# A hybrid attention and convolution layer: the input projection's tokens cut into 272, 256, 256 and 256, and attention begun one gate tile later

## The chip, the cores and the metric

The kernel runs on one core of one Trainium2 chip. The metric is the device time of one execution in microseconds. The engines spoken of are PE (the matrix engine; PEld is its weight load), DVE (vector), ACT (scalar), POOL (GpSimd) and SP (which here only issues DMA transfers). PE adds products up in PSUM, in banks of 512 float32 per partition; DVE or ACT must empty a bank before PE writes to it again.

## The reference, cut to what matters

One layer of width 1024 on 1024 tokens with 16 meta tokens ahead of them (1040 rows in all). All arrays are float32.

```python
h = concatenate([meta, x], axis=1)                    # 1040 x 1024
h = layer_norm(h, in_ln_g, in_ln_b)
z = h @ w_in + b_in                                   # 3840 columns
q, k, v, c_in, gates = split(z)                       # 512, 128, 128, 1024, 2048
a = swa_sink_attention(q, k, v, sinks, rel_bias)      # window 128, 16 meta keys, 8 q heads, 2 kv heads
y_attn = a @ w_attn_proj
c_val, c_gate = split(c_in)
c = causal_dwconv(c_val * sigmoid(c_gate))            # 31 taps
y_conv = silu(layer_norm(c)) @ w_conv_proj
mixed = sigmoid(g_attn) * y_attn + sigmoid(g_conv) * y_conv
h = layer_norm(ALPHA * h + mixed @ w_out)
up = causal_dwconv(h @ ffn_w_up)                      # 3 taps, 2 x 2816 columns
h = layer_norm(ALPHA * h + (gelu(g) * u) @ ffn_w_down)
return h[:, 16:]
```

## The kernel before, in words

**Products in three terms.** A float32 matrix is split into a high part (a copy rounded to the type fp32r) and a low part (what is left, in fp32r), and a product is high x high + high x low + low x high, three matmuls of 128 x 128 weights against a group of token columns. This is `product` (L296): for each of the 8 chunks of the inner dimension, L300, L304 and L305. For the weights ACT makes the high part `whi` (L269) and DVE the low part `wlo` (L272). Two pairs of `whi` and `wlo` take turns.

**The z stage.** z has 30 tiles of 128 columns: q 0 to 3, k 4, v 5, conv values 6 to 9, conv gates 10 to 13, merge gates 14 to 29. Three tiles (one q, k and v) are made first, while the input is still being normalized (L464 to L538, written apart). The other 27 go through `z_tile` (L314): one weight tile, then for each group of tokens `z_group` (L308) takes one of three PSUM banks (tag "mm"), runs the 24 matmuls, and has an evacuation function empty the bank. The groups are the table `HG`, (0, 272), (272, 656), (656, 1040); q tiles and gate tiles use `TG`, the same with the first 14 columns left out, so 258, 384 and 384. Tokens lie in two tiles in SBUF, `RHO` (inner chunks 0 to 3) and `RHC` (4 to 7), each with eight slots, a high and a low one per chunk; `h0` (L255) says where in the tile a slot's columns begin, and the first three tiles, which write these slots, use it too.

**Evacuation.** A conv gate tile: two ACT instructions for each group (L648 and L649, giving a sigmoid by tanh) into one of the staging slots in the tile `FA` (`stage`, L327). A conv value tile: one DVE instruction (L656), which adds the bias and multiplies by the staged sigmoid into `cin`. A q tile: ACT scales into a staging slot (L352) and copies the high part (L354), DVE makes the low part (L355), both go to a scratch array `qd` in DRAM in rows of 64. A merge gate tile: ACT writes tanh into a staging slot (L672), which goes to the scratch array `sgd`.

**Order of the work.** Instructions are written in program order but placed on their engines by a scheduler that goes by priority numbers (`tc.cur_priority`, `rank`) and dependencies; `after(a, b)` adds that a comes behind b. The z tiles come in this order: conv chunk 1 (gate tile 11, value tile 7) and chunk 0, the q tiles, gate tile 0, and then, beside attention, gate tiles 1, 2, conv chunk 2, gate tiles 3, 4, conv chunk 3, gate tiles 5 to 15. Attention goes in 8 blocks of 128 queries for each of 2 kv heads: the queries come back from DRAM as `qt` (a load), PE makes scores (L836), DVE and ACT the softmax, PE transposes (L872) and multiplies with the values (L885). The scheduler lays these between the matmuls of gate tiles. What holds attention's start is `ahead` (L746): the first score product of the meta queries stands behind a chunk of gate tile 0, chosen by number (`first_chunk + 2 * KC + 5`). DVE does the 31 taps of the convolution (L665) where it has time, the residual's multiplications (L447, by the scale of the first layer norm) at the beginning, and the sum of the convolution's channels for its layer norm; PE takes that sum's mean with a ones matrix (`ps_m`, L908 and L909).

After the z stage come the convolution's layer norm, the two projections (L300 to L305 again, into `ps_p`, by groups of 258, 256, 256, 256), the output projection (`ps_w`), the up projection (L1556) and the down projection (L1700).

Of the kernel before, what the change touches and what calls it, by code (L numbers as in the profile page):

```python
# [23 lines left out]
F = mybir.dt.float32  # L24
R = mybir.dt.float32r
# [4 lines left out]
P = 128  # L30
# [25 lines left out]

PG = [(0, 258), (258, 514), (514, 770), (770, 1026)]


# [41 lines left out]
def tile_hybrid_layer(  # L101
# [40 lines left out]
    FA = arena.tile([P, 6144], F, name="FA")  # L142
    RHC = arena.tile([P, 8320], R, name="RHC")
    RHO = arena.tile([P, 8320], R, name="RHO")
    OB = arena.tile([P, 4 * U], F, name="OB")
# [109 lines left out]
    def h0(k, hl, a, b):  # L255
        g = next(g for g, x in enumerate(HG) if a < x[1])
        x, y = HG[g]
        i, n = (k % 4) * 2 + hl, y - x
        o = i * n + ((6144 if i else 0), 272, 3344)[g]
        return (RHO if k < 4 else RHC)[:, o + a - x:o + b - x]  # L260

# [60 lines left out]

    TG = [(a + U0 if i == 0 else a, b) for i, (a, b) in enumerate(HG)]

    st_next = [0]

    def stage(n, lo=4104, cnt=5):  # L327
        i = st_next[0] % cnt
        st_next[0] += 1
        return FA[:, lo + i * 400:lo + i * 400 + n]  # L330

# [310 lines left out]
    def conv_chunk(c):  # L642
        sig = {}

        def g_evac(g, a, b, ps):
            sig[g] = stage(b - a)

            nc.scalar.activation(sig[g], ps, AF.Tanh, bias=bcol(10 + c), scale=0.5)  # L648
            nc.scalar.activation(sig[g], sig[g], AF.Identity, bias=half_, scale=0.5)  # L649

        z_tile(in_cols(10 + c), HG, g_evac, wt_c1[0] if c == 1 else None)
        cin = cp.tile([P, 16 + T], F, name="cin", tag="cin")
        nc.vector.memset(cin[:, 0:16], 0.0)

        def v_evac2(g, a, b, ps):
            nc.vector.scalar_tensor_tensor(cin[:, 16 + a:16 + b], ps, bcol(6 + c), sig[g], OP.add, OP.mult)  # L656

        z_tile(in_cols(6 + c), HG, v_evac2, wt_c1[1] if c == 1 else None)
        with rank(RK_CONV + c * 100):
            for j in range(TAPS):  # L660
                wc = cdw[:, j * CH + c:j * CH + c + 1]
                if j == 0:
                    nc.vector.tensor_scalar(acc[c], cin[:, j:j + U], wc, cdwb(c), OP.mult, OP.add)
                else:
                    nc.vector.scalar_tensor_tensor(acc[c], cin[:, j:j + U], wc, acc[c], OP.mult, OP.add)  # L665
# [79 lines left out]
    gate_tile(0)  # L745
    ahead = chunks_done[first_chunk + 2 * KC + 5]  # L746

# [5 lines left out]
    for h in range(NH):  # L753
# [3 lines left out]
        nc.tensor.matmul(o, pairs0[g][:, 1, r, :], Kx[g][:, 0, 0:16], start=False, stop=True)  # L757
    s2 = ap.tile([P, NH, 16], F, name="s2")
    nc.vector.memset(s2, 0.0)
# [46 lines left out]
    def weights_out(blocks):  # L806
        a, n = 2 * blocks[0], 2 * len(blocks)
        ps = pat.tile([P, 512], F, name="ps_r", tag="t", bufs=2)
        nc.tensor.transpose(ps[:4 * n, :P], rall[:, a:a + n].rearrange("p n h -> p (n h)"), ident)
        t = ap.tile([24, P], F, name="rt", tag="rt", bufs=2)  # L810
        nc.scalar.copy(t[:4 * n], ps[:4 * n, :P])
        for h in range(NH // 2):
            store(dram(rd, 2 * h * S + a * HD, [[HD, n], [S, 2], [1, HD]]),
                  t[h:4 * n:4].rearrange("p (r q) -> p r q", r=2))
# [77 lines left out]
    tc.cur_priority = RK_Z  # L892
    order = [1, 2, "c2", 3, 4, "c3"] + list(range(5, 16))
    for o in order:
# [40 lines left out]
    def temp(n):  # L935
        return tmp_p.tile([P, 386], F, name="t", tag="t", bufs=6)[:, :n]

# [917 lines left out]
```

## Time and profile before

| | |
|---|---|
| median of 3 runs | 1241.26 us (1241.05 to 1242.42) |
| the profiled execution | 1241.21 us |
| its span | 1239.4 us |
| PE busy | 1228.1 us, 8545 matmuls |
| DVE busy | 1084.9 us, 1846 instructions |
| ACT busy | 579.6 us, 1047 instructions |

A profile line in a timeline gives the start from the span's beginning, the duration, engine, source line, operation, output <- inputs, tile shape, and in brackets how long the engine had been idle before it and what released it. Matmuls overlap one another, so their durations add up to more than the time that they take. A line in the list of waits gives the total in us, how often, and the longest. A line in the chain that ended last gives start, length, engine and a number of instructions in a row.

### The profile page before, as it was taken

To read this page: it belongs to the slowest core of one execution; us is meant where nothing else is said; L and a number is where in the kernel's file an instruction comes from. 1 tells how busy PE (TensorE), PEld (TensorE's weight loads), DVE (VectorE), ACT (ScalarE), POOL (GpSimd) and SP (SyncE) were. 2 spreads that over 40 slices of the span, in tenths; PEclk is the share of its full clock that TensorE was granted. 3 is DMA by queue.
4 is the path that set the end of the run, shared out by engine and by line. 5 is a ranking of instruction groups with operands and counts; after the bars stand their busy time and mean duration, and the time that the engine had idled before them with its cause. 6 is when DMAs were issued, how large, how long until landed. Compare 5 with 4: busy or idle time off the path is not lost.

```text
span 1239.4 us, 21709 instructions
## 1 busy us (share of the span) xinstructions
PE 1228.1 (99%) x8545; PEld 1169.1 (94%) x8545; DVE 1084.9 (88%) x1846; ACT 579.6 (47%) x1047; POOL 13.3 (1%) x11
## 2 busy tenths in 40 slices
PE   9999999999999999999999999999999999999997
PEld 8999999999999999888999999999999998888885
DVE  7899989999978798759899999998999986995697
ACT  7522335664255323344755555455454454544330
POOL 0000000000000010000000000000000000000000
PEclk9999999999999999999999999999999999999999
DMA  7296844412264655222145555544455479987722
GB/s 283 67 300 149 194 122 107 122 46 86 80 164 141 177 164 145 102 87 86 52 171 205 204 179 213 184 174 153 162 203 196 174 247 321 387 322 282 255 85 85
DMA packets 109024, 213.08 MB, mean 172 GB/s; under 512 B 31739, under 2 KB 48683, under 8 KB 108794
## 3 DMA queue, kind: packets, MB, share of 16 engines
q1 hardware_dynamic: 93002, 200.63, 49.3%
q10 hardware_dynamic: 15920, 11.07, 3.0%
q8 instruction: 67, 1.10, 0.4%
q14 instruction: 35, 0.29, 0.1%
HBM read 150.04 MB, written 62.70 MB: 172 GB/s over the span
## 4 chain that ended last, share of the span: by engine, by line
PE 96%; DVE 2%; DMA 1%; issue 0%; ACT 0%; SPq 0%; DVEq 0%
PE px L1556 14%; PE py L1556 9%; PE ps_x L1700 9%; PE ps_z L305 8%; PE ps_z L304 8%; PE ps_z L300 8%; PE ps_z L1700 7%; PE pw L1556 5%; PE pz L1556 5%; PE ps_p L300 2%; PE ps_p L304 2%; PE ps_p L305 2%; PE ps_w L305 2%; PE ps_w L304 2%; PE ps_w L300 2%; PE ps_z L514 2%
## 5 line engine op out<-in xcount | busy, mean ns | idle before, releaser
L665 DVE SCALAR_TENSOR_TENSOR FA<-cin,cols,FA 128x1026 f32<-128x1026 f32 x120 | 152.2, 1279 | 0.9
L305 PE MATMUL ps_z<-RHO,wlo 128*128 128x384 f32 (+2 forms) x324 | 104.1, 321 | 0.0
L300 PE MATMUL ps_z<-RHO,whi 128*128 128x384 f32 (+2 forms) x324 | 103.9, 321 | 0.0
L304 PE MATMUL ps_z<-RHO,whi 128*128 128x384 f32 (+2 forms) x324 | 103.9, 321 | 0.0
L305 PE MATMUL ps_z<-RHC,wlo 128*128 128x384 f32 (+2 forms) x324 | 103.8, 320 | 0.0
L304 PE MATMUL ps_z<-RHC,whi 128*128 128x384 f32 (+2 forms) x324 | 103.7, 320 | 0.0
L300 PE MATMUL ps_z<-RHC,whi 128*128 128x384 f32 (+2 forms) x324 | 103.6, 320 | 0.0
L269 ACT CAST whi<-wr 128x1024 fp32r<-128x1024 f32 x37 | 38.9, 1051 | 91.7 <-PE ps_z L304 71.6
L1366 DVE TENSOR_TENSOR RHO<-wr,RHO 128x512 fp32r<-128x512 f32 x92 | 61.9, 685 | 5.2 <-ACT RHO L1365 5.2
L1365 ACT CAST RHO<-wr 128x512 fp32r<-128x512 f32 x92 | 55.3, 619 | 23.3 <-DVE wr L1383 11.4
L300 PEld LDWEIGHTS ps_z<-RHO,whi 128*128 128x128 f32 x324 | 61.0, 188 | 0.1
L300 PEld LDWEIGHTS ps_z<-RHC,whi 128*128 128x128 f32 x324 | 61.1, 189 | 0.0
L304 PEld LDWEIGHTS ps_z<-RHO,whi 128*128 128x128 f32 x324 | 61.0, 188 | 0.0
L305 PEld LDWEIGHTS ps_z<-RHO,wlo 128*128 128x128 f32 x324 | 61.0, 188 | 0.0
L304 PEld LDWEIGHTS ps_z<-RHC,whi 128*128 128x128 f32 x324 | 61.0, 188 | 0.0
L305 PEld LDWEIGHTS ps_z<-RHC,wlo 128*128 128x128 f32 x324 | 61.0, 188 | 0.0
L1383 DVE TENSOR_TENSOR wr<-wr 128x512 f32<-128x512 f32 x88 | 60.2, 684 | 0.2
L272 DVE TENSOR_TENSOR wlo<-wr,whi 128x1024 fp32r<-128x1024 f32 x35 | 42.7, 1219 | 11.5 <-ACT whi L269 11.1
L672 ACT ACTIVATE FA<-ps_z,cols 128x384 f32<-128x384 f32 (+1 forms) x48 | 26.1, 543 | 48.4 <-PE ps_z L305 44.1
L1568 ACT COPY FA<-px 128x514 f32<-128x514 f32 (+2 forms) x23 | 13.1, 571 | 72.1 <-PE px L1556 72.0
L1365 ACT CAST ws<-wr 128x512 fp32r<-128x512 f32 x60 | 36.1, 618 | 19.3 <-DVE wr L1383 10.7
L1556 PE MATMUL px<-OA,RHO 128*128 128x258 f32 (+1 forms) x336 | 43.9, 279 | 0.0
(468 smaller groups left out, 3478.8 us busy)
## 6 DMA issues: line engine op xcount, KB each, us to landing
wr<-in_w_up_dram SPq DMA_DIRECT2D x44, 512.0 KB, 4.9
wr<-in_w_z_dram SPq DMA_DIRECT2D x30, 512.0 KB, 4.4
fd<-FA SPq DMA_DIRECT2D x44, 256.0 KB, 2.4
OB<-in_w_down_dram SPq DMA_DIRECT2D x19, 512.0 KB
qt<-qd SPq DMA_DIRECT2D x28, 256.0 KB, 3.9
sgd<-FA ACTq DMA_DIRECT2D x32, 192.0 KB, 3.0
td<-OB SPq DMA_DIRECT2D x12, 512.0 KB
sums<-fd SPq DMA_DIRECT2D x12, 512.0 KB, 7.0
```

What stands on the lines that cost most here:

```text
L269: ins = nc.scalar.copy(hi, raw)
L272: return (nc.vector if quick else nc.gpsimd).tensor_tensor(lo, raw, f32(hi), OP.subtract)
L300: ins = nc.tensor.matmul(ps, ah, bh, start=i == 0, stop=False)
L304: nc.tensor.matmul(ps, ah, bl, start=False, stop=False)
L305: last = nc.tensor.matmul(ps, al, bh, start=False, stop=i == n - 1)
L665: nc.vector.scalar_tensor_tensor(acc[c], cin[:, j:j + U], wc, acc[c], OP.mult, OP.add)
L672: nc.scalar.activation(t, ps, AF.Tanh, bias=bcol(14 + i), scale=0.5)
L1365: nc.scalar.copy(hi, src)
L1366: ins = nc.vector.tensor_tensor(lo, src, f32(hi), OP.subtract)
L1383: ins = nc.vector.tensor_tensor(*x)
L1556: ins = nc.tensor.matmul(o, x[:, ks], bmat(sub, q, hl, k), start=first and k + j == 0, stop=k == 3 and j == 2, skip_group_check=not first)
L1700: nc.tensor.matmul(banks[i], l[:, ts], r[:, ws], start=first and a and x + k == 0, stop=z and x == len(ops) - 1 and k == 2, skip_group_che ...
```

## The change

- The 27 z tiles made by `z_tile` go by a new table `ZG`, (0, 272), (272, 528), (528, 784), (784, 1040); `TG` is made from it, so 258, 256, 256, 256. The first three tiles and the split of the input keep their groups `HG`.
- In `RHO` and `RHC`, 8448 columns long (8320 before), the first group's slots begin 14 columns later, at 14 + 272 i (and 6208 columns on for slots 3 to 7); the other 768 columns of a slot now lie in one piece, at 880 + 768 i. Before, the two 384s of a slot lay apart.
- `stage` has 7 slots of 286 columns for groups up to 272, and the 5 of 400 for longer ones; the first two small ones lie elsewhere in `FA`.
- Gate tile 1 is written ahead of attention, and `ahead` is a chunk of gate tile 1 (`first_chunk + 4 * KC + 3`).
- Three smaller buffers: the meta queries' scores share the tag of the block scores, `rt` has 1 buffer in place of 2, the temporary of the convolution's layer norm 5 in place of 6.

```diff
+ZG = [(0, 272), (272, 528), (528, 784), (784, 1040)]
...
-    RHC = arena.tile([P, 8320], R, name="RHC")
-    RHO = arena.tile([P, 8320], R, name="RHO")
+    RHC = arena.tile([P, 8448], R, name="RHC")
+    RHO = arena.tile([P, 8448], R, name="RHO")
...
     def h0(k, hl, a, b):
-        g = next(g for g, x in enumerate(HG) if a < x[1])
-        x, y = HG[g]
-        i, n = (k % 4) * 2 + hl, y - x
-        o = i * n + ((6144 if i else 0), 272, 3344)[g]
-        return (RHO if k < 4 else RHC)[:, o + a - x:o + b - x]
+        i = (k % 4) * 2 + hl
+        if a < 272:
+            o = 14 + i * 272 + (6208 if i > 2 else 0)
+        else:
+            o = 880 + i * 768 - 272
+        return (RHO if k < 4 else RHC)[:, o + a:o + b]
...
-    TG = [(a + U0 if i == 0 else a, b) for i, (a, b) in enumerate(HG)]
-
-    st_next = [0]
-
-    def stage(n, lo=4104, cnt=5):
-        i = st_next[0] % cnt
-        st_next[0] += 1
-        return FA[:, lo + i * 400:lo + i * 400 + n]
+    TG = [(a + U0 if i == 0 else a, b) for i, (a, b) in enumerate(ZG)]
+
+    st_next = [0, 0]
+
+    def stage(n):
+        big = n > 272
+        cnt, size = ((7, 286), (5, 400))[big]
+        o = 4136 + st_next[big] % cnt * size
+        if not big and st_next[0] < 2:
+            o = 3240 + st_next[0] * 280
+        st_next[big] += 1
+        return FA[:, o:o + n]
...
-        z_tile(in_cols(10 + c), HG, g_evac, wt_c1[0] if c == 1 else None)
+        z_tile(in_cols(10 + c), ZG, g_evac, wt_c1[0] if c == 1 else None)
...
-        z_tile(in_cols(6 + c), HG, v_evac2, wt_c1[1] if c == 1 else None)
+        z_tile(in_cols(6 + c), ZG, v_evac2, wt_c1[1] if c == 1 else None)
...
     gate_tile(0)
-    ahead = chunks_done[first_chunk + 2 * KC + 5]
+    gate_tile(1)
+    ahead = chunks_done[first_chunk + 4 * KC + 3]
...
-    s2 = ap.tile([P, NH, 16], F, name="s2")
+    s2 = ap.tile([P, 2, 2, KW], F, name="s2", tag="s", bufs=3)
+    s2 = s2.rearrange("p a b c -> p (a b c)")[:, :NH * 16].rearrange("p (h m) -> p h m", m=16)
...
-    order = [1, 2, "c2", 3, 4, "c3"] + list(range(5, 16))
+    order = [2, "c2", 3, 4, "c3"] + list(range(5, 16))
...
-        return tmp_p.tile([P, 386], F, name="t", tag="t", bufs=6)[:, :n]
+        return tmp_p.tile([P, 386], F, name="t", tag="t", bufs=5)[:, :n]
```

How the instructions stand on the engines, at three places. In these listings a row is the source line, the operation, output <- inputs, size, and how many in a row; `ps_z` is a PSUM bank of a z group, `ps_s` one of scores, `kx_731` the keys of one kv head, `OB` and `xn` the residual, `cin` the convolution's input. Line numbers after the change are those of the changed program, where the product's three lines are L302, L306, L307, the scores L844, the residual L453, the split L274 and the value tile's evacuation L662.

PE, at attention's first block scores; before, in gate tile 0's second group:

```order
L305 MATMUL ps_z<-RHC,wlo 128x258
L300 MATMUL ps_z<-RHO,whi 128x384
L304 MATMUL ps_z<-RHO,whi 128x384
L305 MATMUL ps_z<-RHO,wlo 128x384
...
L836 MATMUL ps_s<-kx_731,qt 128x80 x4
L836 MATMUL ps_s<-kx_731,qt 128x144 x4
```

After, in gate tile 1's second group:

```order
L302 MATMUL ps_z<-RHC,whi 128x256
L306 MATMUL ps_z<-RHC,whi 128x256
L307 MATMUL ps_z<-RHC,wlo 128x256
L844 MATMUL ps_s<-kx_731,qt 128x80 x4
L844 MATMUL ps_s<-kx_731,qt 128x144 x4
L302 MATMUL ps_z<-RHC,whi 128x256
```

The scores moved from behind 8 matmuls of gate tile 0's second group to behind 15 of gate tile 1's, one tile of 96 matmuls later. All 1944 matmuls of 256 columns in the z stage stand so: 976 in a run that a 258 group leads, 325 in one that a 272 group leads, 228 behind transposes, 194 behind scores, 83 behind value products, 96 behind products of the projection, the rest behind others.

DVE, at the value tile of conv chunk 1 (the first value tile); before:

```order
L447 TENSOR_TENSOR xn<-xn,gb 128x1024 x2
L447 TENSOR_TENSOR OB<-OB,gb 128x1024 x2
L272 TENSOR_TENSOR wlo<-wr,whi 128x1024
L447 TENSOR_TENSOR OB<-OB,gb 128x1024 x2
L656 SCALAR_TENSOR_TENSOR cin<-ps_z,cols,FA 128x272
L656 SCALAR_TENSOR_TENSOR cin<-ps_z,cols,FA 128x384 x2
L685 CAST kx_731<-FA 128x8x128
```

After:

```order
L453 TENSOR_TENSOR xn<-xn,gb 128x1024 x2
L453 TENSOR_TENSOR OB<-OB,gb 128x1024 x2
L274 TENSOR_TENSOR wlo<-wr,whi 128x1024
L453 TENSOR_TENSOR OB<-OB,gb 128x1024 x2
L662 SCALAR_TENSOR_TENSOR cin<-ps_z,cols,FA 128x272
L662 SCALAR_TENSOR_TENSOR cin<-ps_z,cols,FA 128x256 x2
L691 CAST kx_731<-FA 128x8x128
...
L693 TENSOR_TENSOR kx_732<-FA,kx_732 64x8x128
L693 TENSOR_TENSOR kx_732<-FA,kx_732 64x8x16
L662 SCALAR_TENSOR_TENSOR cin<-ps_z,cols,FA 128x256
L274 TENSOR_TENSOR wlo<-wr,whi 128x1024
```

The residual's multiplications stand ahead of the first evacuation as before; of the now four evacuations, the last stands behind the work on the keys, and a weight split behind it.

ACT, at the q tiles, before and after; `qsh` is the high part, and the DMA rows are stores that ACT issues:

```order
L352 ACTIVATE FA<-ps_z,qb 128x258
L354 CAST qsh<-FA 128x258
L116 DMA qd<-qsh 128x4x64
L352 ACTIVATE FA<-ps_z,qb 128x384
L354 CAST qsh<-FA 128x384
L116 DMA qd<-qsh 128x6x64
```

```order
L358 ACTIVATE FA<-ps_z,qb 128x258
L360 CAST qsh<-FA 128x258
L117 DMA qd<-qsh 128x4x64
L358 ACTIVATE FA<-ps_z,qb 128x256
L360 CAST qsh<-FA 128x256
L117 DMA qd<-qsh 128x4x64
```

A q tile has four such triples now, with transfers of 4 rows of 64 throughout; SP issues the low parts' transfers in the same number. From the first projection product on, the order on every engine is the same but for a few neighbours that changed places.

More of the change, by code (lines that the diff above doesn't have):

```diff
@@ L809, in weights_out @@
         nc.tensor.transpose(ps[:4 * n, :P], rall[:, a:a + n].rearrange("p n h -> p (n h)"), ident)
-        t = ap.tile([24, P], F, name="rt", tag="rt", bufs=2)
+        t = ap.tile([24, P], F, name="rt", tag="rt", bufs=1)
         nc.scalar.copy(t[:4 * n], ps[:4 * n, :P])
```

## The prediction

> **What bounds the kernel now.** I read the profile's page first, then the list of what TensorE (PE) waited for, then PE's timeline around the groups that the change cuts anew, and last VectorE (DVE) and ScalarE (ACT) where they empty PSUM. The page's head, the clock row and the shares of the chain that ended last:
>
> ```profile
> span 1239.4 us, 21709 instructions
> PE 1228.1 (99%) x8545; PEld 1169.1 (94%) x8545; DVE 1084.9 (88%) x1846; ACT 579.6 (47%) x1047; POOL 13.3 (1%) x11
> PEclk9999999999999999999999999999999999999999
> PE 96%; DVE 2%; DMA 1%; issue 0%; ACT 0%; SPq 0%; DVEq 0%
> ```
>
> PE is busy 99% of the span at a full granted clock, and the chain is PE for 96% of it. All that it waited for in the middle of the program:
>
> ```profile
> PE ps_w L538 <- DVE sel L1089: 1.1, 1, 1.1
> PE ps_h L464 <- DVE xn L428: 0.8, 1, 0.8
> PE ps_s L836 <- DMA qt<-qd: 0.4, 1, 0.4
> PE pw L1556 <- DVE OA L1241: 0.4, 1, 0.4
> PE ps_z L511 <- ACT FA L470: 0.3, 1, 0.3
> ```
>
> That is 3.0 us (1.1+0.8+0.4+0.4+0.3), so the time is the number of matmuls times their pace, and a change can act in two ways: through the pace, or through a new wait of PE. The profiled execution took 1241.21 us (span 1239.4); the median of the runs is 1241.26, so a sum against the profile needs no correction.
>
> **The pace of the group sizes.** A single matmul's listed duration is a latency; the pace is the distance between starts, best read from the first rows of two successive groups (start in us, then duration). A gate tile's two 384-column groups, then its 258-column group:
>
> ```profile
> 331.58 0.34 PE L300 MATMUL ps_z<-RHO,whi 128*128 128x384 f32 x1
> ...
> 339.91 0.28 PE L300 MATMUL ps_z<-RHO,whi 128*128 128x258 f32 x1
> ...
> 342.80 0.34 PE L300 MATMUL ps_z<-RHO,whi 128*128 128x384 f32 x1
> ```
>
> Each group is 8 chunks of 3 matmuls. 48 matmuls of 384 columns take 339.91−331.58 = 8.33 us, 173.5 ns each; 24 of 258 take 2.89 us, 120.4 ns each. Nothing in the z stage has 256 columns yet, but the attention projection does, with the same three-term pattern. Its 256s run at two paces:
>
> ```profile
> 425.10 0.28 PE L300 MATMUL ps_p<-OC,whi 128*128 128x256 f32 x1
> ...
> 428.50 0.28 PE L300 MATMUL ps_p<-OA,whi 128*128 128x258 f32 x1
> ...
> 498.74 0.39 PE L300 MATMUL ps_w<-OA,RHC 128*128 128x512 f32 x1
> 498.97 0.28 PE L300 MATMUL ps_p<-OC,whi 128*128 128x256 f32 x1
> ...
> 500.38 0.39 PE L304 MATMUL ps_w<-OA,RHC 128*128 128x512 f32 x1
> ```
>
> Between the first two rows lie 30 matmuls of 256 columns in 3.40 us: 113.3 ns each. Between the last two lie 12 in 1.41 us: 117.5 ns, and these follow a 512. A 512 itself takes 226.7 ns, twice 113.3 (29.93 us for 132 in the chain's row below). In the up projection each 24 are 12 of 258 and 12 of 256 (2.79 us) or 24 of 256 (2.72 us, 113.3 ns), again fast after the 258s:
>
> ```profile
> 654.35 2.79 PE px L1556 x24
> ...
> 668.25 2.72 PE px L1556 x24
> ...
> 1021.69 29.93 PE ps_z L1700 x132
> ```
>
> **Part 1: 768 columns as three 256s in place of two 384s, 27 tiles.** (8 conv tiles, 3 q tiles, 16 gate tiles.) It removes 48 matmuls per tile and adds 72. At the fast pace 72 x 0.1133 = 8.16 us against 8.33: −0.17 us per tile, x27 = −4.5 us, all of it on PE and so on the path. At the slow pace 72 x 0.1175 = 8.46: +0.13 per tile, +3.5 us. At the 258s' own 120.4 ns, the farthest row, 8.67: +0.34, +9.2 us. I take the fast one, because 19 of the 27 tiles lead with a 258 group, as the fast rows of the up projection do, and the z operands follow each other in the projection's order (chunk by chunk, high, low, high). A slow stretch is plausible where 256s resume after a block's score and value matmuls, which I count as 277 of 1944 in the new order: 277 x 4.2 ns = 1.2 us at most, nothing at least; I take +0.5. The eight conv tiles lead with a 272 group, of which no row shows a 256 behind: 8 x 72 x 4.2 ns = +2.4 us if they went slow, zero if fast; I take zero (their 24 matmuls are as steady as a 258 group's, see the 124.6 ns below) and keep 2.4 as a case.
>
> The Trainium skill has a rule that speaks against this part: "TensorE: Matmul & The Clock Gate", section "Back-to-back issue gap", gives the isolated gap of a warm matmul as N/2.4 + 2.5 ns, a fixed sum for each matmul. By it three 256s cost 327.5 ns and two 384s 325.0, which over 24 x 27 triples is an estimated +1.6 us in place of −4.5. The rows above disagree: 1.5 x 113.3 = 170.0 is less than the 173.5 of one 384, and a 512 is no cheaper per column than a 256.
>
> **Part 2: the first group's slots 14 columns later.** The 272 and 258 groups keep their size and read from another column. Their present paces are 120.4 ns above and, at another offset in the up projection, (2.79 − 12 x 0.1133)/12 = 119.2 ns. The 1.2 ns x 456 matmuls (19 tiles) bounds it at ±0.55 us; I take zero. The slots are written by the same copies earlier; longer tiles alone cost no instruction.
>
> **Part 3: one more PSUM evacuation per tile.** 27 more, and 384-column ones become 256. A gate evacuation on ACT and one of the conv value tiles on DVE (the brackets give the idle time before it), and the dense stretch of DVE (its length, then busy time and instructions of PE, weight loads, DVE, ACT and GpSimd, then clock and DMA):
>
> ```profile
> 347.17 0.58 ACT L672 ACTIVATE FA<-ps_z,cols 128x384 f32<-128x384 f32 x1 [1.38 <-PE ps_z L305]
> 78.22 1.01 DVE L656 SCALAR_TENSOR_TENSOR cin<-ps_z,cols,FA 128x272 f32<-128x272 f32 x2
> 190.00:313.00 123.00, 123.00 (x882) 122.38 (x882) 117.49 (x257) 67.76 (x193) 0.00 (x0) 1.00 0.34 92
> ```
>
> In a regular tile it is ready for the bank 0.6 us after its group; three banks take turns, so it has two more groups of time: now 2.89+4.16 or more, afterwards 2 x 2.72 = 5.4 us. That leaves over 4 us of slack, and the added evacuations (under 0.58 us each, 27 x 0.58 = 16 us on an ACT that is idle for 660) lie beside PE; their extra stores to DRAM go out from ACT's and SP's queues with nobody waiting. Price 0, upper bound a wait where the evacuating engine is late, which is the next item. DVE gets 4 more evacuations (conv value tiles) and 3 more splits (q tiles): some 3 us on an engine that in the densest stretch (the last row, 190 to 313 us) is busy 117.49 of 123.
>
> **Part 4: a new wait in the value tile of conv chunk 1.** There DVE evacuates, and it is late already. Its timeline, and PE's first rows of chunk 1's gate tile, of the value tile and of the tile behind it:
>
> ```profile
> 55.22 4.63 DVE L447 TENSOR_TENSOR xn<-xn,gb 128x1024 f32<-128x1024 f32 x4
> ...
> 75.95 2.34 DVE L447 TENSOR_TENSOR OB<-OB,gb 128x1024 f32<-128x1024 f32 x2
> 56.99 0.37 PE L300 MATMUL ps_z<-RHO,whi 128*128 128x272 f32 x1
> ...
> 68.86 0.29 PE L300 MATMUL ps_z<-RHO,whi 128*128 128x272 f32 x1
> ...
> 71.85 0.34 PE L300 MATMUL ps_z<-RHO,whi 128*128 128x384 f32 x1
> ...
> 80.18 0.29 PE L300 MATMUL ps_z<-RHO,whi 128*128 128x272 f32 x1
> ```
>
> The value tile's 272 group (24 matmuls in 2.99 us, 124.6 ns) ends at 71.85, but its evacuation starts at 78.22, when the residual's multiplications (L447, back to back from 55 us, only weight splits and small copies between) are through; it frees the bank at 78.22+0.49 = 78.71. Now the fourth group behind it, the next tile's first, wants that bank at 80.18: 1.5 us to spare. In the changed kernel the fourth group is the value tile's own last: start 68.86−0.17 = 68.69, +2.99 and 2 x 2.72 = 77.12. DVE's order ahead of it is unchanged, so PE waits 78.71−77.12 = +1.6 us. Bounds: 1.0 if DVE comes half a multiplication earlier, 2.0 if the semaphore and the restart cost 0.4. Queued behind the waiting matmul is only PE itself. DVE then does the second and third group at once; the fourth one's evacuation now stands behind the key halves. Their first and last instructions now, with a weight split between:
>
> ```profile
> 80.99 1.55 DVE L685 CAST kx<-FA 128x1024 fp32r<-128x1024 f32 x4
> 82.51 1.20 DVE L272 TENSOR_TENSOR wlo<-wr,whi 128x1024 fp32r<-128x1024 f32 x1
> 84.80 2.77 DVE L687 TENSOR_TENSOR kx<-FA,kx 64x1024 fp32r<-64x1024 f32 x4
> ```
>
> From 80.99 to 84.80+2.77 = 87.57 are 6.6 us, 1.2 of it the split, which the new order puts behind. So the fourth evacuation is through at 78.7 + 0.9 + 5.4 + 0.5 = 85.5, and its bank is wanted three groups on, at 78.7+2.72+2.99+2.72 = 87.1: 1.6 us to spare, no second wait.
>
> **Part 5: attention begins inside the second gate tile.** The first scores now stall PE:
>
> ```profile
> 136.41 5.32 DMA qt<-qd
> ...
> 141.04 0.34 PE L304 MATMUL ps_z<-RHO,whi 128*128 128x384 f32 x1
> 141.77 1.12 PE L836 MATMUL ps_s<-kx,qt 128*128 128x80 f32 x8 [0.39 <-DMA qt<-qd]
> ```
>
> 141.77−141.04 = 0.73 us where the pace is 0.17: 0.56 us lost, because the transfer lands at 136.41+5.32 = 141.73. In the new order a whole tile, about 11 us, stands between, so this goes: −0.55. What is late next: nothing at that place, since the q tiles' splits gain only one small DVE step and one pair of small transfers per half (5.3 us each at most) inside those 11 us. The other end is that DVE and ACT start the softmax 11 us later. The mean of the convolution is where DVE must be done:
>
> ```profile
> 351.86 0.64 PE L909 MATMUL ps_m<-kx,ones_r 128*128 128x258 f32 x3
> 352.18 3.28 DVE L962 TENSOR_TENSOR FA<-FA,ps_m 128x258 f32<-128x258 f32 x8 [5.13 <-PE ps_m L909]
> ```
>
> DVE idles 5.13 us there, waiting for PE, and PE reaches it 4.5−1.6 = 3 us earlier. DVE's work before it is the same but for 3 us; with 5.5 us idle in the dense stretch it fits. Price 0, bounds 0 to +3. The fewer temporary buffers (6 to 5, 2 to 1) and the 16-meta-query scores in a shared buffer: the list of PE's waits has none there, so 0.
>
> **Sum:** 1241.21 − 4.5 + 0.5 + 1.6 − 0.55 = 1238.3 us.
>
> **Rivals.** (a) *All 256s slow* (the other side): the z groups run at 117.5 ns as after a 512. For it: the 384s of the z stage are slower per column than 512s, so something there may hold that the up projection lacks; against it: every 256 behind a 258. It decides at 173.5/1.5 = 115.7 ns. 1241.21+3.5−0.55+1.6 = 1245.8; with a fixed cost as small as +1.6 us for all triples 1243.9. (b) *The gain is eaten in part*: the conv tiles slow (+2.4), or DVE binding between 190 and 350 us (+2 to +3): 1238.3+2.4 = 1240.7. For it, DVE's 117.49 of 123; against, its 5.13 us idle behind. (c) *The new wait does not come*, because DVE's multiplications run earlier or the bank comes from another group: 1238.3−1.6 = 1236.7; against it, DVE's order there is the same. (d) That the cut changes no pace (1.5 x 256 = 384) leaves −0.55+1.6 = +1.0: 1242.3, counted with (b).
>
> **Chances.** Forecast 0.48 (own range 1237.2 to 1239.6), (a) 0.19, (b) with (d) 0.20, (c) 0.13. A difference of 0.2%, 2.5 us, is what a measurement of this kernel can tell from none: faster lies below 1238.8, which holds (c) and two thirds of the forecast, 0.13+0.32 = 0.45; same is the other third and (b), 0.16+0.20 = 0.36; slower is (a), 0.19. The range goes from 1236.2, under (c), to 1245.0, within (a).
>
> **What will show it.** Gate tiles without attention in them should take 2.89+8.16 = 11.05 us (11.22 now); 11.35 is (a). The list of PE's waits should lose the first scores and gain one of 1 to 2 us in ps_z on DVE cin near 77 us. DVE's idle time before the ps_m subtraction should shrink from 5.13 to about 2 us; if PE waits for ps_m or its inputs instead, it is (b). Wrong altogether would be waits of PE on ACT's evacuations, or on qt later in attention.

## The result and the profile after

The changed kernel takes 1244.96 us (median of 7 runs, 1244.67 to 1245.55); the kernel before, beside it on the same chip, 1241.05 us (7 runs, 1240.32 to 1242.42). The ratio is 1.0034 with a 95% interval of 1.0024 to 1.0044: slower by 0.34%, where 0.24% faster was forecast.

The page of the changed kernel's profile, head and clock row:

```profile
span 1243.7 us, 23087 instructions
PE 1228.5 (99%) x9193; PEld 1169.8 (94%) x9193; DVE 1085.9 (87%) x1853; ACT 588.8 (47%) x1078; POOL 13.2 (1%) x11
PEclk9999999999999999999999999999999999999999
```

PE has the 648 additional matmuls, the clock is granted in full, and PE's busy time hardly differs. Where the span grew is told by the first z product of conv chunk 1 and the first product of the projections, of the kernel before (its first row stands in the prediction) and of the changed one:

```profile
409.16 0.28 PE L300 MATMUL ps_p<-OA,whi 128*128 128x258 f32 x1
```

```profile
56.85 0.38 PE L302 MATMUL ps_z<-RHO,whi 128*128 128x272 f32 x1
...
413.56 0.28 PE L302 MATMUL ps_p<-OA,whi 128*128 128x258 f32 x1
```

The z stage, with attention in it, took 409.16−56.99 = 352.17 us and now takes 413.56−56.85 = 356.71: +4.54 us. The stages behind it last the same within 0.1 us. So "the z stage" below means this stretch, and its length is the sharpest measure of an edit.

What PE waited for in the changed kernel:

```profile
PE ps_z L302 <- ACT FA L678: 1.5, 2, 1.2
PE ps_h L470 <- DVE xn L434: 1.4, 1, 1.4
PE ps_z L302 <- DVE cin L662: 1.3, 1, 1.3
PE ps_s L844 <- DMA qt<-qd: 1.1, 1, 1.1
...
```

Against the list of before there are two new lines in the z stage, on ACT (1.5) and on DVE's `cin` (1.3), and the one on `qt` has grown from 0.4 to 1.1. (The line on `xn`, before the z stage, was between nothing and 1.6 us in the kernels below, whose beginning is the same.)

The pace of gate tiles 7 and 8, where nothing lies between the matmuls; first rows of successive groups:

```profile
311.39 0.28 PE L302 MATMUL ps_z<-RHO,whi 128*128 128x256 f32 x1
...
319.87 0.28 PE L302 MATMUL ps_z<-RHO,whi 128*128 128x258 f32 x1
...
322.75 0.28 PE L302 MATMUL ps_z<-RHO,whi 128*128 128x256 f32 x1
...
330.92 0.29 PE L302 MATMUL ps_z<-RHO,whi 128*128 128x258 f32 x1
```

From 311.39 to 319.87 are 72 matmuls of 256 columns in 8.48 us, 117.8 ns each; from 322.75 to 330.92 the next tile's 72 in 8.17 us, 113.5 ns. Slow and fast tiles alternate, from the first q tile (slow) to gate tile 10, wherever attention does not break in. All undisturbed conv tiles, which begin with a 272 group, are fast.

Sorting the distance from each matmul's start to the next start, over the whole z stage, gives this sum (a steady matmul is one behind the first five of its run):

| term | us |
|---|---|
| 1944 x 113.3 ns in place of 1296 x 173.4 ns | −4.5 |
| steady matmuls slower than their fast pace: 256s 3.1, 272s 0.3, less 0.2 for 258s and what the kernel before had | +3.2 |
| first five matmuls of a group or behind another product | +1.4 |
| waits of PE (4.5 in the distances, 0.6 before) | +4.0 |
| the rest, attention's own products among it | +0.4 |
| sum | +4.5 |

So the gain that was forecast from the pace is there, and is given back twice: about 4.6 us by pace and 4.0 by waits.

### The profile page after: what moved, and what is told of

Same layout as the page of the kernel before. It is cut to its first block, busy times and chain, and to the rows that moved or that the text cites. A ratio compares the mean times of both kernels' runs of the same rounds, so it can differ in the third digit from the quotient of the medians.

```text
span 1243.7 us, 23087 instructions
## 1 busy us (share of the span) xinstructions
PE 1228.5 (99%) x9193; PEld 1169.8 (94%) x9193; DVE 1085.9 (87%) x1853; ACT 588.8 (47%) x1078; POOL 13.2 (1%) x11
## 4 chain that ended last, share of the span: by engine, by line
PE 92%; DVE 3%; DMA 2%; ACT 2%; issue 1%; SPq 0%; ACTq 0%; DVEq 0%
PE px L1564 14%; PE py L1564 9%; PE ps_x L1708 9%; PE ps_z L1708 7%; PE ps_z L302 7%; PE ps_z L306 7%; PE ps_z L307 7%; PE pw L1564 5%; PE pz L1564 5%; PE ps_p L302 2%; PE ps_p L306 2%; PE ps_p L307 2%; PE ps_w L307 2%; PE ps_w L306 2%; PE ps_w L302 2%; PE ps_z L520 2%
## 5 line engine op out<-in xcount | busy, mean ns | idle before, releaser
L302 PE MATMUL ps_z<-RHO,whi 128*128 128x256 f32 (+2 forms) x432 | 121.9, 282 | 2.8 <-ACT FA L678 1.5
L307 PE MATMUL ps_z<-RHC,wlo 128*128 128x256 f32 (+2 forms) x432 | 121.7, 282 | 0.0
L307 PE MATMUL ps_z<-RHO,wlo 128*128 128x256 f32 (+2 forms) x432 | 121.6, 282 | 0.0
L302 PE MATMUL ps_z<-RHC,whi 128*128 128x256 f32 (+2 forms) x432 | 121.5, 281 | 0.0
L306 PE MATMUL ps_z<-RHO,whi 128*128 128x256 f32 (+2 forms) x432 | 121.3, 281 | 0.0
L306 PE MATMUL ps_z<-RHC,whi 128*128 128x256 f32 (+2 forms) x432 | 121.3, 281 | 0.0
L302 PEld LDWEIGHTS ps_z<-RHO,whi 128*128 128x128 f32 x432 | 81.8, 189 | 3.4 <-ACT FA L678 1.9
L302 PEld LDWEIGHTS ps_z<-RHC,whi 128*128 128x128 f32 x432 | 81.9, 189 | 0.0
L306 PEld LDWEIGHTS ps_z<-RHC,whi 128*128 128x128 f32 x432 | 81.4, 188 | 0.0
L306 PEld LDWEIGHTS ps_z<-RHO,whi 128*128 128x128 f32 x432 | 81.4, 189 | 0.0
L307 PEld LDWEIGHTS ps_z<-RHO,wlo 128*128 128x128 f32 x432 | 81.4, 188 | 0.0
L307 PEld LDWEIGHTS ps_z<-RHC,wlo 128*128 128x128 f32 x432 | 81.3, 188 | 0.0
L678 ACT ACTIVATE FA<-ps_z,cols 128x258 f32<-128x258 f32 (+1 forms) x64 | 30.2, 473 | 66.2 <-PE ps_z L307 62.6
L274 DVE TENSOR_TENSOR wlo<-wr,whi 128x1024 fp32r<-128x1024 f32 x35 | 42.7, 1219 | 10.4 <-ACT whi L271 9.7
L1374 DVE TENSOR_TENSOR ws<-wr,ws 128x512 fp32r<-128x512 f32 x60 | 40.4, 685 | 4.0 <-ACT ws L1373 3.9
```

The costliest lines, as they stand in the source:

```text
L274: return (nc.vector if quick else nc.gpsimd).tensor_tensor(lo, raw, f32(hi), OP.subtract)
L302: ins = nc.tensor.matmul(ps, ah, bh, start=i == 0, stop=False)
L306: nc.tensor.matmul(ps, ah, bl, start=False, stop=False)
L307: last = nc.tensor.matmul(ps, al, bh, start=False, stop=i == n - 1)
L678: nc.scalar.activation(t, ps, AF.Tanh, bias=bcol(14 + i), scale=0.5)
L1374: ins = nc.vector.tensor_tensor(lo, src, f32(hi), OP.subtract)
```

## The experiments

Each kernel was timed beside the kernel before on the same chip; the table gives both, the ratio with its 95% interval, and the z stage of the profiled execution (352.17 us in the kernel before, 356.71 in the changed one).

| kernel | median, us | before beside it | ratio | z stage, us |
|---|---|---|---|---|
| changed | 1244.96 | 1241.05 | 1.0034 (1.0024 to 1.0044) | 356.71 |
| e1_offset0 | 1245.53 | 1241.00 | 1.0037 (1.0024 to 1.0050) | 356.91 |
| e2_lead | 1244.87 | 1241.00 | 1.0030 (1.0018 to 1.0041) | 354.76 |
| e3_chunk1_hg | 1243.75 | 1241.00 | 1.0024 (1.0015 to 1.0034) | 354.55 |
| e4_gate1_back | 1245.80 | 1241.00 | 1.0042 (1.0030 to 1.0055) | 358.66 |
| e5_q_hg | 1244.07 | 1240.10 | 1.0030 (1.0019 to 1.0041) | 354.70 |
| e6_offset2 | 1244.12 | 1240.10 | 1.0037 (1.0022 to 1.0051) | 355.17 |
| e7_fewer_waits | 1240.44 | 1240.10 | 1.0004 (0.9994 to 1.0013) | 351.75 |
| e8_held | 1240.21 | 1240.10 | 1.0000 (0.9991 to 1.0010) | 351.36 |
| e9_spare_banks | 1241.24 | 1240.42 | 1.0004 (0.9995 to 1.0013) | 352.10 |
| e10_all_three | 1240.99 | 1240.42 | 1.0004 (0.9996 to 1.0013) | 352.20 |
| e11_and_leads | 1239.63 | 1240.42 | 0.9993 (0.9984 to 1.0002) | 350.53 |
| e12_more_leads | 1238.75 | 1240.41 | 0.9985 (0.9976 to 0.9994) | 350.61 |

The kernels ran on several chips, and the kernel before took 1240.10 to 1241.05 us beside them, so medians are best compared as distances to it: +3.9 us for the changed kernel. The expectations' times are worked out from 1244.96 us, that is beside 1241.05. The ratios of e1 to e6 overlap with that of the changed kernel, so their medians do not tell them apart from it; what they show is in their traces, one execution of each. e7 to e12 are clear of the changed kernel.

The theory was that the pace of a 256 is a state carried from group to group, and that three late arrivals (DVE, the queries, ACT), each brought by the finer cut, make the waits. The rivals: that the slow pace belongs to a place (column, weight buffer, bank), and that the waits come from attention's later begin.

### The first group's slots back at column 0

```diff
-            o = 14 + i * 272 + (6208 if i > 2 else 0)
+            o = i * 272 + (6208 if i > 2 else 0)
```

> The changed kernel (1244.96 us) with the first group's slots 14 columns earlier again (at 272 i, and 6208 columns on for slots 3 to 7); nothing else moves on any engine. Theory A (phase): a 256 runs at 113.3 or 117.8 ns according to the state in which the group ahead ended, and each 258 group turns one state into the other, so tiles alternate; the column offset only sets the 272 groups' pace, which goes from 127.7 back to 124.6 ns (192 x 3.1 ns = 0.6 us): 1244.4 us, tiles still alternate. Rival B (place): the slow state comes from the 258 groups' new column, so all 256s become fast: 1.551 thousand steady 256s lose their 3.1 us, and with the 272s it takes 1241.3 us.

First rows of groups in e1_offset0, a conv tile's 272 and its first 256, then gate tile 7's 256s:

```profile
69.25 0.28 PE L302 MATMUL ps_z<-RHO,whi 128*128 128x272 f32 x1
...
72.25 0.28 PE L302 MATMUL ps_z<-RHO,whi 128*128 128x256 f32 x1
...
311.11 0.28 PE L302 MATMUL ps_z<-RHO,whi 128*128 128x256 f32 x1
...
319.58 0.28 PE L302 MATMUL ps_z<-RHO,whi 128*128 128x258 f32 x1
```

Neither came out. The 272 group is back at 3.00/24 = 125 ns, as theory A had it (at column 14 it was 127.7). But the alternation is gone the wrong way: gate tile 7 takes 8.47 us, tiles 8 and 9 as much, and most 256s are slow, also in three of the four conv tiles ahead of the q tiles; slow steady 256s cost 4.7 us in place of 3.1. So the column of the group ahead does decide the state in which the 256s run, and the 14 columns of the change are worth 1.6 us of pace here. The time hardly moves (z stage +0.2) because the waits and the 272s got shorter by about as much.

### A short matmul ahead of each gate tile's second group

```diff
+        product(ps[:, :b - a], [...],
+                lead=h0(0, 0, a, a + 64) if a == 272 and lead_on[0] else None)
...
+        lead_on[0] = True
         z_tile(in_cols(14 + i), TG, gate_evac)
+        lead_on[0] = False
```

> The changed kernel with one matmul of 64 columns more ahead of the second group of each of the 16 gate tiles (its result is overwritten). Theory A (phase): the interruption resets the state, every gate tile's 256s run at 113.3 ns after a few; 8 slow tiles get 0.3 us each back (2.4), and 16 interruptions cost 0.13 us each (2.1, from the projection's lead: 33 ns and a first 256 of 199 ns): 1244.7 us. Rival C (weight buffers or PSUM banks, which alternate from tile to tile too): slow tiles stay slow, and the interruptions are paid: 1247.0 us.

The same two gate tiles in e2_lead, from the short matmul to the next tile:

```profile
311.49 0.19 PE L300 MATMUL ps_z<-RHO,whi 128*128 128x64 f32 x1
311.51 0.36 PE L302 MATMUL ps_z<-RHO,whi 128*128 128x256 f32 x1
...
319.76 0.29 PE L302 MATMUL ps_z<-RHO,whi 128*128 128x258 f32 x1
...
322.65 0.19 PE L300 MATMUL ps_z<-RHO,whi 128*128 128x64 f32 x1
...
330.93 0.29 PE L302 MATMUL ps_z<-RHO,whi 128*128 128x258 f32 x1
```

8.27 and 8.28 us including the short matmul: both fast, in the same weight buffers and banks as in the changed kernel, where they took 8.48 and 8.17. That rejects the rival with buffers and banks, and shows the state as something that an interruption resets. (In one of the 16 gate tiles, between attention's products at 235 us, the 22 matmuls behind the short one were slow even so.) What the state gives, 1.5 us of slow steady 256s, the interruptions take (about 0.11 us each: 8.28−8.17). That the median, 1244.87 us, is near the 1244.7 expected is in part luck: in this execution the waits for ACT and for the queries were 1.1 and 0.7 us shorter, which is most of the 1.95 us by which the z stage is shorter, and 1.2 us came back behind the z stage, 0.7 of it as waits in the down projection.

### Conv chunk 1 by the old groups

```diff
-        z_tile(in_cols(10 + c), ZG, g_evac, wt_c1[0] if c == 1 else None)
+        z_tile(in_cols(10 + c), HG if c == 1 else ZG, g_evac, wt_c1[0] if c == 1 else None)
...
-        z_tile(in_cols(6 + c), ZG, v_evac2, wt_c1[1] if c == 1 else None)
+        z_tile(in_cols(6 + c), HG if c == 1 else ZG, v_evac2, wt_c1[1] if c == 1 else None)
```

> The changed kernel with conv chunk 1's two tiles by the old groups 272, 384, 384. The wait of the value tile on DVE's evacuation (1.3 us at 78.6) goes; two tiles go back from three fast 256s to two 384s (+0.33): 1244.0 us. Rival: the tiles behind then wait for the same late DVE (as the next tile would for its bank), and the time stays at 1245.0 or above.

The head of PE's waits in e3_chunk1_hg:

```profile
PE ps_z L302 <- ACT FA L678: 1.8, 2, 1.2
PE py L1564 <- ACT OB L1576: 1.2, 1, 1.2
...
```

Behind these are only lines from ahead of the z stage. The wait for DVE is gone and the z stage is 2.2 us shorter, since the wait for the queries went with it. The q tiles are cut here as in the change, so their cut alone does not bring that wait. In this execution 1.2 us came back as a wait in the up projection, far behind the edit; a similar one, 1.4 us, shows in e5. What brings it was not pursued. The median, 1243.75, is close to the 1244.0 expected.

### Attention's begin as before

```diff
-    gate_tile(1)
-    ahead = chunks_done[first_chunk + 4 * KC + 3]
+    ahead = chunks_done[first_chunk + 2 * KC + 5]
...
-    order = [2, "c2", 3, 4, "c3"] + list(range(5, 16))
+    order = [1, 2, "c2", 3, 4, "c3"] + list(range(5, 16))
```

> The changed kernel with gate tile 1 written behind attention again and the meta queries' scores held by a chunk of gate tile 0's third group, as before. If the later begin of that part is what made the waits for the queries (1.1 us at 144) and for ACT (1.5 us at 378 and 385), both go: 1242.4 us. If they come from the cut into more groups, they stay, and it takes 1244.5 to 1245.5 us.

The three waits of the z stage in e4_gate1_back:

```profile
PE ps_z L302 <- ACT FA L678: 1.8, 1, 1.8
PE ps_z L302 <- DVE cin L662: 1.3, 1, 1.3
PE ps_s L843 <- DMA qt<-qd: 1.1, 1, 1.1
```

All three are there, none smaller, and the time is above the range given for this case (1245.8). So the waits come from the cut, not from the moved gate tile. The z stage of this execution is 1.95 us longer than the changed kernel's, and the granted clock explains 1.7 of them. It dropped right behind the wait of 1.8 us on ACT (columns as in the prediction's row of the dense stretch, the clock third from the end):

```profile
386.02:389.43 3.41, 3.41 (x18) 3.41 (x18) 3.22 (x9) 1.16 (x3) 0.00 (x0) 0.50 0.76 187
```

For 3.41 us the clock was half, and the 256s there lie 213 ns apart; elsewhere in the z stage it was granted in full, and slow steady 256s cost 3.1 us, as in the changed kernel. So moving the gate tile changed the pace neither way. That the wait brought the clock down is not shown: the changed kernel waited 1.2 us at the same place and kept it.

### The q tiles by the old groups

```diff
-        z_tile(in_cols(r), TG, q_evac(r))
+        z_tile(in_cols(r), THG, q_evac(r))
```

(`THG` is `HG` without its first 14 columns.)

> The changed kernel with the three q tiles by the old groups 258, 384, 384. Theory (cut): three groups more to evacuate, split and send per q tile are what makes the queries late, so PE's wait for them falls from 1.1 to about 0.4 us (-0.7), while the three tiles' pace changes by less than 0.3 us: 1244.3 us. Rival: the wait depends on when PE gets there alone, and stays at 1.1: 1245.0 us.

```profile
PE ps_s L845 <- DMA qt<-qd: 0.2, 1, 0.2
```

PE's wait for the queries falls from 1.1 to 0.2 us, as the theory has it. But it was gone in e3 too, and is in e7 below, both with the q tiles cut in four, so this run does not show their cut as the cause. The z stage loses 2.0 us rather than 0.7: slow steady 256s cost 1.2 us less (two of the changed kernel's slow tiles are q tiles), and the wait on ACT is 0.4 us shorter. The median is no nearer to the kernel before (+4.0), with 1.4 us back in the up projection.

### The first group's slots at column 2

```diff
-            o = 14 + i * 272 + (6208 if i > 2 else 0)
+            o = 2 + i * 272 + (6208 if i > 2 else 0)
```

> The changed kernel with the first group's slots beginning at column 2 + 272 i in place of 14 + 272 i, so that the 258 groups begin on a multiple of 16 columns, as in the projections, where every 256 behind them ran at 113.3 ns. If the column decides how a group leaves the pace of those behind it: all 256s behind 258 groups fast (-3.1 us of slow steady matmuls, nearly all), 1242.0 us; the conv tiles' 272 groups at column 2 are not known, and if they leave their 256s slow that is +2.3. If the state only flips at each 258 group, whatever its column: 1245 us.

A conv tile, then gate tile 8, in e6_offset2:

```profile
96.44 0.28 PE L302 MATMUL ps_z<-RHO,whi 128*128 128x256 f32 x1
...
104.92 0.28 PE L302 MATMUL ps_z<-RHO,whi 128*128 128x258 f32 x1
...
321.87 0.29 PE L302 MATMUL ps_z<-RHO,whi 128*128 128x256 f32 x1
...
330.04 0.28 PE L302 MATMUL ps_z<-RHO,whi 128*128 128x258 f32 x1
```

Gate tile 8 now takes 8.17 us, and tiles 7 and 9 as much: behind the 258s nothing alternates. The conv tile takes 8.48: the 272 group at column 2 leaves the 256s at the slow pace. Slow steady 256s cost 2.1 us (3.1 in the changed kernel), 1.2 of it in the four conv tiles ahead of the q tiles, so the place as such was worth 1.0 us of pace. The median does not show it: it is 4.0 us above the kernel before, as the rival's 1245 us would be. Until here a place that is always fast behind a 258 would do as well as a state; e10 decides.

### Without the waits: old groups at four tiles, the scores held

```diff
+        z_tile(in_cols(14 + i), THG if i in (12, 13) else TG, gate_evac)
...
+                        if not i:
+                            after(ins, held)      # e8 alone
+    held = chunks_done[first_chunk + 2 * KC + 2]
```

Both have the slots at column 2 and chunk 1 by the old groups.

> As the kernel before it in this list (slots from column 2), and conv chunk 1's two tiles and gate tiles 12 and 13 by the old groups 272 or 258, 384, 384. The waits for DVE (1.3 us at 78.6) and ACT (1.5 us at 378 and 385) go, four tiles cost 0.17 to 0.3 us more: 1.9 us below that kernel, so 1240.1 us if its 256s are fast, 1243.0 if not. Rival: the waits only move to tiles behind, no gain.

> As the kernel before it, and the scores of attention's first block held behind a chunk of gate tile 0's third group, 16 matmuls of 256 later (1.8 us). PE's wait for the queries (1.1 us at 144 in the changed kernel) goes: 1.0 us below that kernel, 1239.1 us if the 256s are fast. Rival: the later softmax brings a new wait of the same size further on: no gain.

In e7_fewer_waits none of the lines on ACT, `cin` and `qt` is left in PE's list, and with 1240.44 us it is 0.3 us above the kernel before. That the expected 1240.1 us was nearly met is luck: it was worked out for fast 256s and a gain of 1.9 us over e6, but slow steady 256s still cost 1.7 us, and the z stage gained 3.4 us, since the wait for the queries went with the other two. In e8_held nothing is left to gain by holding the scores, and 0.2 us is what the median moved, so this run says little on holding them.

### Without the waits: a fourth bank

```diff
     def z_group(wt, g, a, b, evac, spare=None):
         hi, lo = wt
-        ps = pat.tile([P, 512], F, name="ps_z", tag="mm", bufs=3)
+        tag, bufs = spare if spare and g == 3 else ("mm", 3)
+        ps = pat.tile([P, 512], F, name="ps_z", tag=tag, bufs=bufs)
...
+        z_tile(in_cols(6 + c), ZG, v_evac2, ..., ("s", 2) if c == 1 else None)
...
+        z_tile(in_cols(14 + i), TG, gate_evac, spare=("o", 1) if i in (11, 12, 13) else None)
```

> The changed kernel (1244.96 us) with all groups as cut, but a PSUM bank that is idle at the time taken for the fourth group of conv chunk 1's value tile (one of the scores' banks) and of gate tiles 11, 12 and 13 (the attention output's bank), so that four banks take turns there. If a late evacuation and three banks are the cause of the waits on DVE (1.3 us) and ACT (1.5 us): both go, 1242.2 us. If PE's earlier arrival lets the wait for the queries at 144 us grow by what was won at 78 us: 1243.5 us. Rival: the waits come from something else than the bank: 1245.0 us.

PE's waits in e9_spare_banks:

```profile
...
PE ps_s L845 <- DMA qt<-qd: 0.5, 1, 0.5
...
```

With every tile cut as in the change and the slots at column 14, the lines on `FA` L678 and `cin` are gone from the list, and the time is 1241.24 us, 0.8 us above the kernel before in place of 3.9: the waits were most of the slowdown. That is 0.3 us better than expected (1242.2 beside 1241.05), and the wait for the queries shrank too. For the value tile the bank is the cause: DVE begins that evacuation no earlier than in the changed kernel (78.80 us, 78.10 there), and PE no longer waits for it. On ACT the scheduler also laid the table loads differently, so there the bank is not shown alone.

### Everything together, and short matmuls where the pace is slow

```diff
 # e10: slots at column 2, a fourth bank, the scores held
 # e11: and
         sig = {}
+        lead_on[0] = c < 2
...
+        lead_on[0] = False
 # e12: and
+        lead_on[0] = i in (1, 12)
         z_tile(in_cols(14 + i), TG, gate_evac, ...)
+        lead_on[0] = False
```

> The kernel before it with slots from column 2 + 272 i and the first block's scores held 16 matmuls longer: every tile cut as in the change, none of the three waits, and the 258 groups leaving a fast state. Against 1244.96 us: -1.3, -1.5 and -1.1 us of waits and about -2.0 us of slow steady 256s: 1239.1 us, below the kernel before. If the pace alone cannot pay for the cut, it stays at 1241 or above.

> As e10, and a matmul of 64 columns ahead of the second group of the four conv tiles of chunks 1 and 0, whose 272 groups (at column 2) leave a slow state: 4 x (0.32 - 0.12) = 0.8 us less, 1238.3 us. Rival: the interruption costs what it saves, 1239.1 us.

> As e11, with the matmul of 64 columns also ahead of the second group of gate tiles 1 and 12, which run slow in e11 (2 x 72 x 4.4 ns lost): 2 x (0.32 - 0.12) = 0.4 us less, 350.1 us for the z stage (350.5 in e11; 352.2 in the kernel before) and 1.2 us below the kernel before. Rival: the interruptions move the scheduler's order around attention, and other tiles fall into the slow state for it: the z stage takes 350.5 us or more.

Two tiles in e10_all_three, with the slots at column 2 as in e6: the first q tile, then gate tile 8:

```profile
106.73 0.29 PE L302 MATMUL ps_z<-RHO,whi 128*128 128x256 f32 x1
...
114.90 0.28 PE L302 MATMUL ps_z<-RHO,whi 128*128 128x258 f32 x1
...
319.91 0.28 PE L302 MATMUL ps_z<-RHO,whi 128*128 128x256 f32 x1
...
328.39 0.28 PE L302 MATMUL ps_z<-RHO,whi 128*128 128x258 f32 x1
```

The q tile takes 8.17 us, gate tile 8 takes 8.48, and gate tiles 7 and 9 as much: the same column, behind a 258 group each time, gives both. In e6 attention's last product left the 256s at the fast pace, here at the slow one, and the 258 groups behind it hand on the pace that they find. So a pace is carried on, and the place alone does not set it. The pace ahead does not set it alone either: the q tile above is fast behind a conv tile whose 256s were slow. The 258s tell the two cases apart: 24 of them take 2.89 us behind the conv tile and 2.85 us between slow gate tiles.

It cost e10 its gain: no wait in the z stage, 3.6 us of slow steady 256s, and 0.6 us above the kernel before where 2.0 below was expected. e11 has 1.3 us of them left and the shortest z stage, 350.53 us; its ratio still reaches 1. The short matmuls gave 0.8 us of that gain and cost some 0.4 themselves; 1.8 us came behind attention, where gate tiles 7 to 9 and 13 to 15 happened to be fast again. e12 has 0.6 us left; in its profiled execution the wait for the queries is back with 0.4 us, and the z stage is not shorter than e11's, as its rival had it. Its runs are nevertheless the only ones clear of the kernel before: 1238.75 against 1240.41 us, 0.9985 (0.9976 to 0.9994), 1.7 us where 1.2 was expected. Which part of it the two further short matmuls brought is not shown.

## Why the prediction was wrong

**The pace (part 1), mis-sized.** −4.5 was right as the price of fast 256s. The step that failed is the choice that all 256s behind a 258 group are fast, read from the attention and up projections. In the up projection 12 and 24 matmuls stand behind 258s at another column. In the attention projection, where the 113.3 ns was first read, the run of 256s does not stand right behind the 258s; the kernel before has a matmul of 64 columns between them:

```profile
412.05 0.19 PE L298 MATMUL ps_p<-OA,whi 128*128 128x64 f32 x1
412.08 0.36 PE L300 MATMUL ps_p<-OA,whi 128*128 128x256 f32 x1
```

That is the interruption that e2 copied, and it leaves the fast pace. The rows of before could not show that the state is handed on. Slow steady 256s took 3.1 us where 0.5 was set, of the 8.0 us that lie between all fast (−4.5) and all slow (+3.5). (The 0.5 counted the 256s behind scores and value products; the 228 behind transposes, listed in the part on the change, were left out.) Conv tiles, kept as a case, were fast.

**What the sum left out.** The first matmuls behind a change of size or behind another product cost 1.4 us more; no term had them. The 14 columns (part 2) were set to zero with a bound of 0.55; on the 272s alone they cost about 192 x 2.5 ns = 0.5 us, from 125.0 ns in e1 to the 127.5 ns (3.06/24) of this pair of rows of the changed kernel, but their larger effect was on the state.

```profile
93.16 0.29 PE L302 MATMUL ps_z<-RHO,whi 128*128 128x272 f32 x1
...
96.22 0.28 PE L302 MATMUL ps_z<-RHO,whi 128*128 128x256 f32 x1
```

**The evacuations on ACT (part 3), wrong.** "Over 4 us of slack" was worked out from a stretch where ACT had little else. Where the convolution's layer norm runs, ACT's rows of before and of the changed kernel are these:

```profile
372.19 2.09 ACT L995 ACTIVATE FA<-FA,cols 128x258 f32<-128x258 f32 x4
374.18 0.56 ACT L672 ACTIVATE FA<-ps_z,cols 128x384 f32<-128x384 f32 x1
```

```profile
372.63 2.09 ACT L1003 ACTIVATE FA<-FA,cols 128x258 f32<-128x258 f32 x4
374.74 1.28 ACT L991 ACT_TABLE_LOAD   x1
376.03 0.58 ACT L991 ACTIVATE t<-ps_m,eps 128x384 f32<-128x384 f32 x1
376.63 1.28 ACT L678 ACT_TABLE_LOAD   x1
377.93 0.47 ACT L678 ACTIVATE FA<-ps_z,cols 128x256 f32<-128x256 f32 x1
...
379.72 1.28 ACT L991 ACT_TABLE_LOAD   x1 [0.39 <-ACT FA L678]
...
381.62 1.28 ACT L1003 ACT_TABLE_LOAD   x1
...
385.08 0.45 ACT L678 ACTIVATE FA<-ps_z,cols 128x256 f32<-128x256 f32 x1
```

```profile
385.58 0.39 PE L302 MATMUL ps_z<-RHO,whi 128*128 128x256 f32 x1 [1.15 <-ACT FA L678]
```

Before, an evacuation stood right behind the swish activations (L995). Now it stands behind two more table loads and an activation, at 377.93, 3.2 us after the swish ended; ACT is busy from 372.63 to 378.40, 5.8 us and longer than the two groups of 2.7 us for which three banks last, and PE waits 0.3 us. The longer wait, 1.15 us, comes two groups later: the evacuation that it needs starts at 385.08, again behind two table loads, with activations and a weight cast between, and PE's matmul starts when it is through. The Trainium skill ("ScalarE: Activation LUTs", section "What ACT_TABLE_LOAD costs") gives 1283 ns for such a load, which these rows show, and 1380 ns of draining beside it, which they don't: the activation starts 0.01 us after the load, and the loads at 374.74 and 376.63 start 0.02 us after the instruction ahead of them. The prediction named waits of PE on ACT's evacuations as what would make it wrong altogether; they cost 1.5 us.

**The value tile of conv chunk 1 (part 4), right.** Here is PE's row and DVE's evacuation of the three groups in the changed kernel:

```profile
78.10 1.26 DVE L662 SCALAR_TENSOR_TENSOR cin<-ps_z,cols,FA 128x272 f32<-128x272 f32 x3
78.63 0.39 PE L302 MATMUL ps_z<-RHO,whi 128*128 128x256 f32 x1 [1.30 <-DVE cin L662]
```

PE was to wait until 78.71 for 1.6 us; it waited until 78.63, for 1.3. e3, without the fourth group, and e9, with a fourth bank, confirm the mechanism.

**Attention's begin (part 5), wrong.** The place was misread, in the part on the change too: the first block's scores stand in gate tile 0's second group in both kernels. The groups ahead of them in the order's listing are three q tiles and gate tile 0, and the first gate evacuation of the changed kernel is that tile's:

```profile
141.28 0.48 ACT L678 ACTIVATE FA<-ps_z,cols 128x258 f32<-128x258 f32 x1 [1.14 <-PE ps_z L307]
```

`ahead` holds the meta queries' scores alone. So no tile stands between the queries and the scores, and PE comes there at nearly the same point of the program. The chain that brings the queries ends so in the changed kernel:

```profile
133.75 5.14 DMA qd<-qsl
139.62 4.29 DMA qt<-qd
```

The store of the low parts takes 5.14 us (3.27 before) and the queries land at 143.91 us in place of 141.73; the stall became 1.1 us, +0.7 where −0.55 was set. What makes them late stays open: e5 took the cut of the q tiles back and the wait fell to 0.2, but e3 and e7 kept that cut and have no wait, and e9 kept it with 0.5.

**The rest.** DVE idled 3.24 us before the ps_m subtraction (5.13 before, about 2 foretold) and was not the bound: rivals (b) by DVE and (c) did not come. (a), the case on the slow side, named 1243.9 to 1245.8 us, which holds the measured time, but not by its mechanism: less than half of its pace came, and waits that it did not contain made up the rest, so that is luck. The rule of the Trainium skill that the prediction weighed ("TensorE: Matmul & The Clock Gate", section "Back-to-back issue gap") gave an estimated +1.6 us in place of −4.5 by a fixed cost of each matmul. The fast tiles above (8.17 us for 72) don't bear it out, and neither price knows of two paces for one size.

## What to carry to other kernels

A group size that is cheap per column in one stage can run at a second pace in another, depending on the groups ahead of it; price it with both, and read the pace of whole groups in the new program before counting the gain. More and smaller groups with the same number of banks shorten the time in which an evacuation may be late, so look for the stretch where the evacuating engine is busiest, not for the regular one. To say where a moved product stands, count the tiles ahead of it by their evacuations, and check which instruction a dependency really holds.

## What the runs showed of the hardware that was not expected

- Matmuls of 256 columns on a PE that never idles have two steady paces, 113.3 and 117.8 ns, at the same granted clock (gate tiles 7 and 8 of the changed kernel, in full), and keep one until a group of another size or another product intervenes.
- What a group of 24 matmuls hands on depends on where it starts reading (columns of the first slot; the others lie 272 further each). 258 columns from column 28 turned the state over all 11 times in the changed kernel, though in e3, e4 and e5 a slow one also stayed slow; from 16 they kept it behind attention (e6, e10), but turned slow to fast behind a slow conv tile, and at one place of e11 and e12; from 14 they mostly left it slow (e1). 272 from column 14 left it fast, from 0 and 2 slow (e1, e6).
- A matmul of 64 columns between groups takes 0.03 us to the next start and makes the 256 behind it 85 to 92 ns longer. It left those behind it at the fast pace in e2, e11 and e12, but for one place beside attention in e2.
- Behind a wait of PE of 1.8 us in e4 the granted clock was half for 3.41 us, which cost 1.7 us; a wait of 1.2 us in the changed kernel had no such effect.
- Why the column matters was not settled: the runs tell which columns do what, not through what part of the engine.
